# A one-core 4096 x 4096 matmul with leaky ReLU: when a21's pieces are turned, where s3's quarter sums lie, and leaky on two row tiles at once

## The chip, the core and the metric

The kernel runs on one core of a Trainium2 chip. TensorE multiplies (128 rows of the contraction at a time, into PSUM banks of 128 x 512 fp32), VectorE adds, subtracts, transposes 32 x 32 blocks and applies leaky ReLU, ScalarE copies PSUM banks to SBUF and squares blocks for a check, and the queues of GpSimd (POOL), SyncE (SP) and ScalarE issue transfers. The metric is the device time of one execution in microseconds. Three runs of the kernel before took 1546.32 to 1549.6 us, median 1548.78.

## The reference

```python
def reference(a, b, alpha):            # a, b: 4096 x 4096 float32, alpha = 0.01
    x = np.matmul(a, b)
    return np.where(x > 0, x, alpha * x)
```

## The kernel before

The output is cut into four row groups g (1024 rows) and four column blocks j (1024 columns), so 16 regions of 1024 x 1024. Region (0,0) is made by an ordinary product while data comes in. Each of the other fifteen, in the list `regions` (L489), is made by Winograd's form of Strassen's scheme: `a` and `b` of the region are split into 2 x 2 blocks, and seven products of sums replace eight. `PRODUCTS` (L636) names their left sides in order: a11, a12, s2, s3, s1, a22, s4. In the text, product 0 is a11, product 3 is s3, product 6 is s4. One such product is 64 matmuls of 128 x 512 (four row tiles, two halves k of the contraction, eight chunks). The order within a group is j = 2, 0, 1, 3, in group 2 it is 2, 0, 3, 1, and in group 0 it is 1, 2, 3.

The sums on the `b` side (t1 to t4, L571) are made in place on VectorE in every region. Those on the `a` side (s1, s2, s3, s4, L541) are made once per group, and s3 lies in the room of a21.

In most regions of groups 1 to 3 the last two products, and product 3 from a group's second region on, are split once more: seven quarter products of 16 matmuls of 128 x 256 replace 64 matmuls by 112 half-wide ones (L735). Their left sides need four quarter sums each. For a22 and s4 these are made in the group's first region and kept in DRAM (`kept_q`). For s3 they are made in the group by `sums_of_s3` (L708): sums 1 and 3 at the end of the first region, 2 and 4 in the second one (L996), in the rooms of quarters that are not needed meanwhile (`s3_rooms`, the x21 quarters of a22, s4 and s3), the fourth in a small tile and then in DRAM (`kept_s3`). From the second region on the fourth is loaded (L1060) into `t`, a tile that takes the room of s2 after product 2. The quarter sums of `b` for product 3 (`tq`: 2, 4 and 1) are made after product 1, in three small tiles (tag a16, of which there are three).

The last region of a group (`turning`: (0,3), (1,3) and (2,1)) is not made in quarters. In it the next group's `a` is fetched and turned: a11 after product 0, a12 after product 1 or 2, a21 after product 3, a22 after product 5, each block in four pieces. A piece is fetched by four casting transfers on POOL into an a16 tile (L131), turned by two 32 x 32 transposes on VectorE (L140) and squared on ScalarE by four instructions that also sum (L590); the row sums feed a check of the input's range (`note_rows`, L596). The squares of blocks of `b` (`Measure`, L229 to L262) feed the same check: three squares on ScalarE in `begin`, and in `end` a sum on VectorE, a fourth square, two more sums and a fold of five small steps. In (1,3) and (2,1) the block B22 is measured in the room of the next group's s2 (`IN_ROOM`). Since the quarter sums have overwritten x21 of a22, s4 and s3, these three quarters are reloaded from DRAM there (`load_x21`, L706).

What is done with the results: after product 0 ScalarE copies the y banks to u1 (L798), after product 1 VectorE adds the z banks (L942), makes the four row tiles leaky (L309) and SP stores them (L947): that is `leave`. After product 2 the y banks, which go on accumulating, are copied to u2. After product 3 the z banks are copied to v; after product 4 the y banks are added to v, which then leaves; after product 5 the z banks are added to u2; after product 6 the y banks are copied to kept_c (L1154) and leave. Products 5 and 6 go on accumulating in z and y, and the next region's products 0 and 1 start anew in the banks z and y of this one.

The schedule is written out by hand: each engine's queue runs its instructions in the order of the program's text and waits at semaphores. SP's order in a turning region is: u1's stores, x21 of s3, the loads of the next region's B12 (for groups 2 and 3 its finished sum t3), x21 of a22 and s4, v's stores, then the next region's B11 (two loads, L512), its B21, u2's stores, its B22, kept_c's stores. In the regions with j = 2 of groups 1 to 3, `b` is read from a 16-bit copy in DRAM (`kept`) on SP; in the others it comes from the input with a cast, on POOL (L515). ScalarE's copies of the z banks after product 3 stand behind the squares of a12's pieces.

## Time and profile before

| what | us |
|---|---|
| median of three runs (lowest to highest) | 1548.78 (1546.32 to 1549.6) |
| profiled execution, its own time | 1553.42 |
| its span, first to last instruction | 1551.6 |
| TensorE busy | 1528.9 (99%) |
| VectorE busy | 1148.7 (74%) |
| ScalarE busy | 425.1 (27%) |
| POOL busy | 300.4 (19%) |

The granted TensorE clock is 0.998 over the span. DMA moved 341 MB, mean 220 GB/s. In the rows of a timeline the columns are: start in us, length in us, engine and line, operation, output and inputs, shapes, count, and in brackets the engine's idle time before the row and what ended it. In the list of waits the columns are: who, what ended the wait, us in total, times, the longest. A group's row gives busy us and the mean ns of one instruction.

### The profile page before, as it was taken

How to read it: one execution, taken by the hardware profiler on the slowest of the kernel's cores; microseconds unless marked ns; L12 is line 12 of the kernel's file. 1: busy time of each engine (PE TensorE's matmuls, PEld its weight loads, DVE VectorE, ACT ScalarE, POOL GpSimd, SP SyncE). 2: the span in 40 equal slices, each digit the busy share in tenths (PEclk: the TensorE clock that was granted, in tenths of full speed). 3: DMA queues.
4: the chain of work that ended last, by engine and by line, in shares of the span. 5: the costliest groups of instructions: out<-in, count | busy, mean ns of one | idle time of the engine just before them, and what ended most of it. 6: DMA issues, size and time to landing. Idle time of an engine off the chain costs nothing. (4 is left out here: it accounts for less than half of the span.)

```text
span 1551.6 us, 21870 instructions
## 1 busy us (share of the span) xinstructions
PE 1528.9 (99%) x8571; PEld 836.8 (54%) x8571; DVE 1148.7 (74%) x1318; ACT 425.1 (27%) x730; POOL 300.4 (19%) x482
## 2 busy tenths in 40 slices
PE   9999999999999999999999999999999999999997
PEld 4444444444446466574444747557444475747656
DVE  4368768777797787966789698675869868787686
ACT  2201224646310214104651130311473113021310
POOL 5641110144102011023400202012340110201100
PEclk9999999999999999999999999999999999999999
DMA  9999695999879989599997979969999795979933
GB/s 244 182 215 199 129 286 156 180 197 187 271 279 276 217 189 277 145 267 201 230 305 252 282 175 228 240 166 274 207 204 342 201 282 138 273 193 189 273 109 139
DMA packets 218163, 341.30 MB, mean 220 GB/s; under 512 B 19137, under 2 KB 162753, under 8 KB 210114
## 3 DMA queue, kind: packets, MB, share of 16 engines
q0 software_dynamic: 149376, 141.59, 57.3%
q1 hardware_dynamic: 62050, 172.65, 30.3%
q10 hardware_dynamic: 6624, 25.56, 4.4%
q8 instruction: 69, 1.13, 0.3%
q14 instruction: 44, 0.36, 0.1%
HBM read 375.92 MB, written 103.29 MB: 309 GB/s over the span
## 5 line engine op out<-in xcount | busy, mean ns | idle before, releaser
L785 PE MATMUL ps<-b,a 128*128 128x512 f16 x2752 | 599.5, 379 | 6.0 <-DMA a<-kept_xs 4.4
L785 PE MATMUL ps<-b,s 128*128 128x512 f16 x2240 | 489.2, 379 | 1.4 <-DVE b L571 1.4
L785 PEld LDWEIGHTS <-a 128*128 128x128 f16 x2752 | 269.0, 98 | 330.2 <-DMA a<-kept_xs 5.3
L785 PEld LDWEIGHTS <-s 128*128 128x128 f16 x2240 | 219.1, 98 | 264.4 <-issue 1.8
L515 POOL DMA_DIRECT2D b<-in_b_dram x184 | 136.6, 747 | 920.1 <-PE ps L735 442.3
L571 DVE TENSOR_TENSOR b<-b 128x4096 f16<-128x4096 f16 x104 | 234.5, 2288 | 78.3 <-DMA b<-in_b_dram 70.9
L798 ACT COPY c<-ps 128x512 f32<-128x512 f32 x152 | 78.5, 596 | 452.6 <-PE ps L785 437.1
L140 DVE STREAM_TRANSPOSE a<-a 128x512 uint32<-128x512 uint32 (+2 forms) x120 | 126.8, 1105 | 92.3 <-DMA a<-in_a_dram 92.2
L131 POOL DMA_DIRECT2D a<-in_a_dram x252 | 137.8, 553 | 206.0 <-ACT junk L590 86.8
L590 ACT ACTIVATE junk<-a 128x512 bf16<-128x512 f16 x192 | 121.3, 632 | 111.4 <-DMA a<-in_a_dram 106.0
L309 DVE SCALAR_TENSOR_TENSOR c<-c 128x512 f32<-128x512 f32 x240 | 149.5, 686 | 3.1 <-ACT c L1154 3.0
L735 PEld LDWEIGHTS <-q 128*128 128x128 f16 x1392 | 135.8, 98 | 17.5 <-DMA q<-kept_s 1.6
L942 DVE TENSOR_TENSOR c<-ps,c 128x512 f32<-128x512 f32 x142 | 88.9, 683 | 59.6 <-PE ps L785 50.2
L229 ACT ACTIVATE sq<-b 128x2048 bf16<-128x2048 f16 x56 | 104.4, 1910 | 59.9 <-DVE sq L238 40.1
L281 PE MATMUL ps<-b,a 128*128 128x512 f16 x512 | 113.1, 379 | 2.4 <-DMA b<-in_b_dram 1.2
L735 PEld LDWEIGHTS <-a 128*128 128x128 f16 x1040 | 101.8, 98 | 15.4
L735 PE MATMUL ps<-b,q 128*128 128x256 f16 x752 | 88.2, 273 | 0.8 <-DMA q<-kept_s 0.8
L281 PEld LDWEIGHTS <-a 128*128 128x128 f16 x512 | 49.7, 98 | 63.7 <-issue 4.0
L883 ACT COPY c<-ps 128x512 f32<-128x512 f32 x9 | 5.3, 587 | 268.6 <-PE ps L735 148.3
L735 PE MATMUL ps<-b,a 128*128 128x256 f16 x656 | 77.2, 273 | 0.0
L836 DVE TENSOR_TENSOR c<-ps,c 128x512 f32<-128x512 f32 x80 | 52.3, 685 | 14.6 <-PE ps L735 14.6
L735 PEld LDWEIGHTS <-s 128*128 128x128 f16 x592 | 57.9, 98 | 6.7
(113 smaller groups left out, 892.0 us busy)
## 6 DMA issues: line engine op xcount, KB each, us to landing
b<-in_b_dram POOLq DMA_DIRECT2D x192, 512.0 KB, 13.5
out_dram<-c SPq DMA_DIRECT2D x240, 256.0 KB, 6.5
a<-in_a_dram POOLq DMA_DIRECT2D x244, 128.0 KB, 5.4
b<-kept SPq DMA_DIRECT2D x20, 1024.0 KB, 9.3
q<-kept_qs ACTq DMA_DIRECT2D x40, 512.0 KB, 7.9
s<-kept_s SPq DMA_DIRECT2D x18, 1024.0 KB, 6.4
q<-kept_qa SPq DMA_DIRECT2D x28, 512.0 KB, 7.3
b<-in_b_dram POOLq DMA_DIRECT2D x24, 256.0 KB, 9.3
```

Of the source, the lines that this page charges most:

```text
L131: nc.gpsimd.dma_start(a16[32 * q:32 * q + 32], src.rearrange("(g i) w -> i g w", i=32))
L140: nc.vector.transpose(part.rearrange("p c m e -> p c (m e)").bitcast(U32) .rearrange("p c (g i) -> p g c i", i=32), src[:, :, i * n:(i + 1 ...
L229: nc.scalar.activation(to, self.parts[n], SQUARE)
L281: nc.tensor.matmul(ps, a_cols(at[0, h, u], c, mt, (h, u) == (0, 0)), bt[0, u, nt][:, c, :], start=first, stop=last,)
L309: nc.vector.scalar_tensor_tensor(t, t, alpha, t, op0=MULT, op1=MAX if alpha <= 1 else MIN)
L515: nc.gpsimd.dma_start(t[:, c:c + 4, :], b_rows(j, u, c, 4, nt, g > 0))
L571: nc.vector.tensor_tensor(f(to), f(x0), f(x1), op)
L590: nc.scalar.activation(junk, piece[:, q, :], SQUARE, accum_out=to[:, 4 * n + q:4 * n + q + 1])
L735: nc.tensor.matmul(to[m], xq[:, c // 2, rows, c % 2], yq[:, c, :], start=first and c == 0 and m < banks, stop=c == KC - 1, skip_group_chec ...
L785: nc.tensor.matmul(banks[mt], a_cols(t, c, mt, t is first_a), B(half, nt, k)[:, c, :], start=first and (k, c) == todo[0], stop=(k, c) == t ...
L798: nc.scalar.copy(kept[mt], banks[mt])
L942: nc.vector.tensor_add(to, bank, to)
```

## The change

It has these parts.

- `leave` takes pairs of row tiles (a tile of 128 x 2 x 512) and makes both leaky in one instruction of 128 x 1024; the two stores stay separate. The addition of v to u2 in the quartered regions goes by pairs too.
- s3's fourth sum no longer goes through `t`. In a group's second region it is made after product 1 in an a16 tile (`sx4`), stored in DRAM and used from there; in later regions it is loaded into such a tile behind u1's stores. The second sum is made ahead of the early measures of that region.
- The quarter sum t1 moves from an a16 tile to `t`, and is made after product 2.
- In (1,3) and (2,1), s3's x21 is loaded before a11's pieces are fetched, ahead of u1's stores in SP's queue.
- In a turning region a21's pieces 3 and 4 are fetched with the others, but turned and squared after v has left. In (1,3) and (2,1) the measure of B22 moves from behind product 4 to behind product 3: its three squares stand ahead of piece 1, its end between pieces 1 and 2, and the rooms of the next s2 and s1 are taken in this order.
- a22's piece 4 is turned ahead of the sums s1 and s2 as before, but squared after product 6's copies, which now use `keep`.

```diff
-    def sums_of_s3(g, some):
+    def sums_of_s3(g, some, room=None):
...
             if n == 4:
-                sx[4] = by_chunk(new_a16())
+                sx[4] = by_chunk(room)
...
-                nc.sync.dma_start(by_chunk(kept_s3), sx[4])
+                nc.sync.dma_start(kept_s3, room)
...
-        def leave(acc, h, nt):
-            for mt, t in enumerate(acc):
-                leaky(t)
-                nc.sync.dma_start(place(g, h, mt, j, nt), t)
+        def leave(pairs, h, nt):
+            for r, t in enumerate(pairs):
+                leaky(t.rearrange("p m n -> p (m n)"))
+                for m in range(2):
+                    nc.sync.dma_start(place(g, h, 2 * r + m, j, nt), t[:, m, :])
...
-        def fetch_a(h, half, some=slice(None)):
-            if not turning:
-                return
-            for n in range(MT)[some]:
-                if n == 0:
-                    coming["rows", h, half] = small_pool.tile([P, 16], FP32, name="rows", tag=f"rows{half}")
-                fetch, turn = coming[h, half][n]
-                fetch()
-                turn()
-                square_rows(turn.held[0], n, coming["rows", h, half])
-                if n == MT - 1:
-                    rows_made.append(coming["rows", h, half])
+        def fetch_a(h, half, n):
+            if n == 0:
+                coming["rows", h, half] = small_pool.tile([P, 16], FP32, name="rows", tag=f"rows{half}")
+            coming[h, half][n][0]()
+
+        def square_a(h, half, n):
+            square_rows(coming[h, half][n][1].held[0], n, coming["rows", h, half])
+            if n == MT - 1:
+                rows_made.append(coming["rows", h, half])
+
+        def bring_a(h, half, some=range(MT)):
+            if turning:
+                for n in some:
+                    fetch_a(h, half, n)
+                    coming[h, half][n][1]()
+                    square_a(h, half, n)
...
         product(0, y, True)
+        if second_of_group:
+            sums_of_s3(g, (2,))
         for n, m in enumerate(early):
             if n:
                 m.begin()
             m.end()
-        if second_of_group:
-            sums_of_s3(g, (2, 4))
...
-        fetch_a(0, 0, slice(3 if g else None))
+        if turning and g:
+            load_x21(g, "s3")
+        bring_a(0, 0, range(3 if g else 4))
 
         product(1, z, True)
         add(u1, z)
-        leave(u1, 0, 0)
+        leave(u1_pairs, 0, 0)
...
         if in_fourth:
-            tq = {n: new_a16() for n in (2, 4, 1)}
+            tq = {n: new_a16() for n in (2, 4)}
+            sx4 = new_a16()
+            if not second_of_group:
+                nc.sync.dma_start(sx4, kept_s3)
             t3_of_b(quarters_of_b(i, 0, 1))
-            sums_of_b(quarters_of_b(i, 0, 1), tq)
+            sums_of_b(quarters_of_b(i, 0, 1), tq, (2, 4))
+            if second_of_group:
+                sums_of_s3(g, (4,), sx4)
...
-        if turning:
-            load_x21(g, "s3")
...
         u2_pairs, u2 = keep(y, 1 - side)
+        if in_quarters:
+            t = x_pool.tile([P, 4, QUARTER], DT, name="q", tag="x")
+        if in_fourth:
+            tq[1] = t[:, 3]
+            sums_of_b(quarters_of_b(i, 0, 1), tq, (1,))
...
-        if in_quarters:
-            t = x_pool.tile([P, 4, QUARTER], DT, name="q", tag="x")
-            if in_fourth:
-                nc.sync.dma_start(t[:, 3], kept_s3)
...
-        fetch_a(1, 0)
-        note_rows(1)
+        in_room = None
         if turning:
+            room = new_s(g + 1, "s2").rearrange("p k c m e -> p (k c m e)").bitcast(BF16)
+            if (g, j) in IN_ROOM:
+                in_room = measure(i, *IN_ROOM[g, j], room.rearrange("p (n w) -> p n w", n=4))
+                in_room.begin()
+            bring_a(1, 0, [0])
+            if in_room:
+                in_room.end()
+            bring_a(1, 0, [1])
+            for n in (2, 3):
+                fetch_a(1, 0, n)
             load_x21(g, "a22")
             load_x21(g, "s4")
...
-            for mt in range(MT):
-                nc.vector.tensor_add(u2[mt], u2[mt], v[mt])
+            for to, more in zip(u2_pairs, v_pairs):
+                f = lambda t: t.rearrange("p m n -> p (m n)")
+                nc.vector.tensor_add(f(to), f(to), f(more))
...
         product(4, y, False)
-        in_room = None
         if turning:
             new_s(g + 1, "s1")
-            t = new_s(g + 1, "s2").rearrange("p k c m e -> p (k c m e)").bitcast(BF16)
-            if (g, j) in IN_ROOM:
-                in_room = measure(i, *IN_ROOM[g, j], t.rearrange("p (n w) -> p n w", n=4))
-                in_room.begin()
...
             add(v, y)
-            leave(v, 1, 1)
-        if in_room:
-            in_room.end()
-        note_rows()
+            leave(v_pairs, 1, 1)
+        if turning:
+            for n in (2, 3):
+                coming[1, 0][n][1]()
+                square_a(1, 0, n)
+            note_rows(1)
...
-        fetch_a(1, 1, slice(3))
-        leave(u2, 1, 0)
+        bring_a(1, 1, range(3))
+        leave(u2_pairs, 1, 0)
...
-        fetch_a(1, 1, slice(3, None))
         if turning:
+            note_rows()
+            fetch_a(1, 1, 3)
+            coming[1, 1][3][1]()
             for name in ("s1", "s2"):
                 sum_a(g + 1, name)
...
-            _, kept_c = new_c(side)
-            for mt in range(MT):
-                nc.scalar.copy(kept_c[mt], y[mt])
+            kept_c, _ = keep(y, side)
+            if turning:
+                square_a(1, 1, 3)
             leave(kept_c, 0, 1)
```

## The prediction

> **What bounds the kernel now.** I read the busy table first, then TensorE's list of waits, then TensorE's timeline product by product, then the other engines' timelines in the two regions where most is lost.
>
> ```profile
> PE 1528.9 (99%) x8571; PEld 836.8 (54%) x8571; DVE 1148.7 (74%) x1318; ACT 425.1 (27%) x730; POOL 300.4 (19%) x482
> ```
>
> TensorE is the bound, and the change removes no matmul. So all it can win is TensorE's idle time, which its waits name (who, for what: us in total, times, longest):
>
> ```profile
> PE ps L785 <- DMA a<-kept_xs: 4.4, 2, 2.5
> PE ps L785 <- DVE b L571: 1.4, 1, 1.4
> ...
> PE ps L785 <- DMA b<-kept: 0.9, 1, 0.9
> ...
> PE ps L735 <- DMA q<-kept_s: 0.8, 2, 0.5
> PE ps L785 <- ACT c L1154: 0.3, 1, 0.3
> ```
>
> The timeline gives each wait its place. In region (2,1), where group 3's `a` is turned, products 3, 4, 5, 6 and the next region's product 0 begin thus:
>
> ```profile
> 1112.65 7.50 PE L785 MATMUL ps<-b,a 128*128 128x512 f16 x34
> 1122.66 6.65 PE L785 MATMUL ps<-b,a 128*128 128x512 f16 x30 [2.51 <-DMA a<-kept_xs]
> 1129.15 13.98 PE L785 MATMUL ps<-b,s 128*128 128x512 f16 x64
> 1142.96 13.98 PE L785 MATMUL ps<-b,a 128*128 128x512 f16 x64
> 1156.78 13.98 PE L785 MATMUL ps<-b,s 128*128 128x512 f16 x64
> 1171.68 18.52 PE L785 MATMUL ps<-b,a 128*128 128x512 f16 x85 [0.93 <-DMA b<-kept]
> ```
>
> An undisturbed product takes 13.81 us from start to start (1129.15 to 1142.96), in quarters 12.23. What exceeds that is lost: product 3 of (2,1) 2.69, of (1,3) 2.02, both for s3's x21; product 0 of (3,2) 1.09, for `b<-kept`; around product 1 of (2,2) 1.33, for the copies of L1154; product 2 of (2,0) 1.52, for the sums of L571; product 3 of (1,0), (1,1), (3,0) 0.15, 0.66, 0.48, for the fourth sum read back. Together 9.9 us, 0.6%. Last, what VectorE, ScalarE and SyncE's queue do behind product 3 of (2,1):
>
> ```profile
> 1139.83 2.03 ACT L798 COPY c<-ps 128x512 f32<-128x512 f32 x4
> 1155.11 7.30 ACT L229 ACTIVATE s<-b 128x2048 bf16<-128x2048 f16 x4
> ```
> ```profile
> 1151.12 2.10 DVE L140 STREAM_TRANSPOSE a<-a 128x512 uint32<-128x512 uint32 x2 [0.41 <-DMA a<-in_a_dram]
> 1153.15 0.30 DVE L596 TENSOR_TENSOR stats<-stats,rows 128x16 f32<-128x16 f32 x3
> 1153.38 2.47 DVE L942 TENSOR_TENSOR c<-ps,c 128x512 f32<-128x512 f32 x4
> 1155.77 2.48 DVE L309 SCALAR_TENSOR_TENSOR c<-c 128x512 f32<-128x512 f32 x4
> ...
> 1162.44 1.23 DVE L241 TENSOR_TENSOR s<-s 128x2048 bf16<-128x2048 bf16 x1 [0.57 <-ACT s L229]
> ...
> 1166.08 0.34 DVE L262 TENSOR_TENSOR stats<-stats,r 128x16 f32<-128x16 f32 x3
> ```
> ```profile
> 1156.47 2.67 SPq L947 DMA_DIRECT2D out_dram<-c  x4
> 1159.38 2.47 SPq L512 DMA_DIRECT2D b<-kept  x4
> ```
>
> The reader should see a chain: v is added and made leaky (L942, L309), only then can its stores issue, and only behind them in the queue the loads of B11 that product 0 of the next region waits for.
>
> **The change, part by part.** The sum is made against the profiled execution (span 1551.6, its time 1553.4 us), which lies 4.6 us above the median 1548.78; I carry the difference over to the median.
>
> *s3's x21 earlier, (1,3) and (2,1).* Its four loads leave their place behind u1's stores (issued at 734.4 and 1114.8) and follow s2's reload at 713.7 and 1093.1, 20 us earlier. With the observed 7.8 to 12.1 us to landing they are there before product 3 starts (733.7, 1112.65). Gain 2.02 + 2.69, if nothing takes its place. Price: 0.5 MB beside the fetches of a11's pieces; at the 408 GB/s of the busiest stretch that is 0 to 1.3 us for those. Their turns feed u1's last addition, ready at 731.3 and needed at 734.3: the 3 us cover it. Beyond that cover product 3 would start late by the rest.
>
> *The squares of a22's last piece behind the copies of product 6.* In (1,3) the copies ran at 804.7, after squares whose piece landed at 801.7, while product 6 ended at 791. Put ahead, they run some 10 us earlier: gain 1.33.
>
> *The B22 measure and a21's last two pieces.* This is the part that decides. Before, VectorE turned all four pieces, then added v and made it leaky, and the measure came last (the rows above). Now v has ahead of it: piece 1, the whole measure, piece 2; only pieces 3 and 4 go behind. The work in front grows a little: two pieces less (4.2 us), against three sums of 1.23 and a fold of 2.7 us (L241's end to L262's). But the measure waits for ScalarE, whose order is now: the copies of z (756.60 + 2.03 in (1,3), 1139.83 + 2.03 in (2,1); they stand behind the squares of a12's last piece, which waits for its landing), three squares of B22 (three quarters of 7.30, 5.5), piece 1's squares (3.0), the fourth square (1.9). So L241 runs 10.4 us after z's copies, at 769.0 and 1152.3. Then 4.0 to the fold's end, 2.1 for piece 2, 2.4 for the additions, 1.2 for the first leaky pair: the first store of v issues 9.7 later, at 778.7 and 1162.0, where it stood at 775.85 and 1156.47. It is 2.9 and 5.5 us later, although TensorE now comes 2.0 and 2.7 us sooner.
>
> Behind these stores wait the loads of B11. Product 0 takes first the half that is loaded second; in (2,1) it was released 15.1 us after v's first store (1156.5 to 1171.6), in (0,3), with no other fetching, it landed 12.9 after (389.8 to 402.7). Less of a22 is now being fetched meanwhile, so I take 13.5: 792.2 and 1175.5. The landing of a12's last piece also shifts, since the second t3 load now issues 2.0 and 2.7 us earlier and meets its fetch: 0 to +2, I take +0.9 and +0.5. Product 0 then starts at 793.1 in (2,2) and 1176.0 in (3,2). Before it was 790.97 and 1171.68: +2.1 and +4.3. In this the x21 gains and the 1.09 are already swallowed; z's copies, which would hold product 5 of (2,1) by 1 us (1140.4 to 1141.9 against a start of 1140.3), hide in the same wait. With the copies' 1.33 off, the turning regions together cost +0.8 +4.3 = +5.1. Ends: with 12.9 and no shift +2.5, with 15.1 and +2 and +1 +9.9.
>
> The Trainium skill, "DMA: Bandwidth & Descriptors", section "Anatomy of one DMA", fits a transfer as 2.0 us plus bytes over 436 GB/s (for GpSimd's path). An estimate from it: the two halves land some 6.8 us after issue, near 10.5 after v's first store, and the turning regions would come to about -0.9 instead of +5.1. The trace disagrees: its loads of this kind take 6.3 to 17.0, median 9.3.
>
> In (0,3) there is no such measure; v comes earlier and product 0 of (1,2) has 11 us to spare: 0.
>
> *The fourth sum and t1.* (2,0): the fourth sum's 1.23 leaves the chain ahead of the sums of L571; the second sum only moves to the front of the same ScalarE-fed measures. Product 2 gains 1.2 of 1.5. (1,0), (1,1): the sum stays in its room, or is loaded from behind u1's stores, one product earlier: 0.15 + 0.66 gained. (3,0): VectorE is late there for another reason (the b load that landed at 1289.65), and u1's addition starts at 1301.49. Behind it now: 2.4, leaky 2.3, t3 and two sums 3.75, the fourth sum: ready at 1311.1, needed by the third quarter product at 1306.65 + 3.5 = 1310.1. Then two L571 of 2.2 and t1, ready 1316.8, needed 1316.4. Lost 1.0 + 0.4 instead of 0.48: +0.9. In other regions t1 is ready before its place (+8.7 in product 3); at worst 1.2 each. Sum -1.1, between -2.5 (all gained) and +1.
>
> *leaky and u2 + v in pairs.* One 128x1024 costs 1.23 (the row of L309 on `part`) for two of 0.69 that overlap to 1.20 (four in 2.49). About 0.07 a pair saved on VectorE, 8 us in all, off the path; first stores of a leave issue 0.5 later, counted above. 0, at most 1 either way. The three reads of kept_s3 that go, and the moved row statistics: 0.
>
> Sum: +5.1 - 1.1 = +4.0, rounded with 0.2 for the pairs to +4.2: 1553.0 us.
>
> **Rivals.** *All stalls go (the other side).* If a12's last piece landed 3 us earlier in (1,3) and 7 to 8 in (2,1), v's stores would go out at 775.5 and 1154.4 and B11 be there in time. Then 2.02 + 2.69 + 1.09 + 1.33 + 1.1 = 8.2 are won: 1540.6. For it: 0.5 MB no longer load beside a12's pieces (734 to 746, DMA share 1.08). Against: that piece's fetch waits for a room that VectorE's turn frees at 746.5, whatever the load.
>
> *The loads are quicker.* (0,3)'s first half landed 7.3 us after issue behind its stores. If the second half now does, 11 after the first store, product 0 starts at 790.6 and 1173.5; the sum is -0.4 - 1.3 + 1.8 - 1.1 = -1.0: 1547.8. The Trainium skill's fit ("DMA: Bandwidth & Descriptors", "Anatomy of one DMA") is of this kind. Against: four loads and four stores then share the engines as before.
>
> *More contention.* The upper ends hold: +9.9 and +1: 1559.7. For it: the window 1164 to 1172 already runs at a DMA share of 1.01.
>
> **How the numbers follow.** Forecast case 0.50, its own range 1550 to 1556; all stalls go 0.20; quicker loads 0.17; more contention 0.13. No change means within 3.1 us (0.2%), about what a measurement can tell. Faster: 0.20 + 0.04 from quicker loads. Same: 0.13 + 0.09 from the forecast's lower part. Slower: the rest, 0.54. The range 1542 to 1559 cuts the outer half of the first and of the last rival.
>
> **What would show it.** Right: in (1,3) and (2,1) product 3 is one row of 64 without a wait; VectorE's L942 follows L262 and two turns; TensorE waits 3 to 8 us for `b<-kept` at product 0 of (2,2) and (3,2); L571's 1.4 shrinks to about 0.3; product 3 of (3,0) waits for VectorE's L718 and L674. Wrong: no wait on `b<-kept`, or v's stores before 776 and 1157.

## The result and the profile after

The changed kernel takes 1564.02 us (median of five runs, 1562.19 to 1566.1) against 1548.78 (1546.32 to 1549.6): 1.010 times as long, with a 95% interval of 1.0086 to 1.0115. The forecast was 1553.0, with a range of 1542 to 1559. So it is slower, as forecast, but by 15.2 us instead of 4.2, outside the range. The profiled execution after took 1564.15 us (span 1562.4).

The busy table of the changed kernel shows no more matmuls than before. TensorE is busy 6 us longer with the same 8571:

```profile
PE 1535.1 (98%) x8571; PEld 838.1 (54%) x8571; DVE 1138.7 (73%) x1179; ACT 424.3 (27%) x730; POOL 300.4 (19%) x482
```

Its list of TensorE's waits (what ended them: us in total, times, longest) has lost x21 (`a<-kept_xs`), L571 and the fourth sum's load (`q<-kept_s`), and has two new heads:

```profile
PE ps L785 <- DVE c L942: 7.3, 5, 3.3
PE ps L785 <- ACT c L798: 4.6, 4, 2.2
...
PE ps L785 <- DMA b<-kept: 0.4, 1, 0.4
...
PE ps L735 <- DVE q L718: 0.3, 1, 0.3
```

TensorE's timeline in (2,1) of the changed kernel, products 3, 4, 5, 6 and the first two of (3,2):

```profile
1115.70 13.98 PE L785 MATMUL ps<-b,a 128*128 128x512 f16 x64
1129.51 13.98 PE L785 MATMUL ps<-b,s 128*128 128x512 f16 x64
1145.67 14.79 PE L785 MATMUL ps<-b,a 128*128 128x512 f16 x64 [2.18 <-ACT c L798]
1163.80 0.38 PE L785 MATMUL ps<-b,s 128*128 128x512 f16 x1 [3.34 <-DVE c L942]
...
1165.59 15.01 PE L785 MATMUL ps<-b,s 128*128 128x512 f16 x61 [0.22 <-DVE c L942]
1180.96 13.99 PE L785 MATMUL ps<-b,a 128*128 128x512 f16 x64 [0.36 <-DMA b<-kept]
1195.87 14.79 PE L785 MATMUL ps<-b,a 128*128 128x512 f16 x64 [0.92 <-ACT c L798]
```

Product 3 is one row without a wait, as forecast. But product 6 waits 3.34 us for L942, the four additions of v, and then again before its second, third and fourth matmul. The reason is in the code: `add(v, y)` reads the y banks, and product 6 accumulates in those same banks. It may not write a bank until VectorE has read it. VectorE's timeline shows why the additions are late:

```profile
1146.00 2.10 DVE L140 STREAM_TRANSPOSE a<-a 128x512 uint32<-128x512 uint32 x2 [1.51 <-DMA a<-in_a_dram]
1150.72 1.23 DVE L238 TENSOR_TENSOR s<-s 128x2048 bf16<-128x2048 bf16 x1 [2.62 <-ACT s L229]
...
1157.19 1.23 DVE L241 TENSOR_TENSOR s<-s 128x2048 bf16<-128x2048 bf16 x1 [3.45 <-ACT s L229]
...
1160.84 0.34 DVE L262 TENSOR_TENSOR stats<-stats,r 128x16 f32<-128x16 f32 x3
1161.10 2.07 DVE L140 STREAM_TRANSPOSE a<-a 128x512 uint32<-128x512 uint32 x2
1163.09 2.45 DVE L942 TENSOR_TENSOR c<-ps,c 128x512 f32<-128x512 f32 x4
```

Piece 1 of a21 is turned at 1146.00; then come the measure's sums, which wait for ScalarE's squares; then piece 2; then the additions. VectorE is idle for most of 1148 to 1157. ScalarE in the same stretch: z's copies, behind the squares of a12's last piece, then B22's squares (its squares of a21's piece 1 lie in the gap between the last two rows):

```profile
1145.05 2.03 ACT L798 COPY c<-ps 128x512 f32<-128x512 f32 x4
1146.95 5.54 ACT L229 ACTIVATE s<-b 128x2048 bf16<-128x2048 f16 x3
...
1155.26 1.90 ACT L229 ACTIVATE s<-b 128x2048 bf16<-128x2048 f16 x1
```

POOL's timeline shows a second effect. There are three a16 rooms for pieces, and a room is free only when VectorE has turned and ScalarE has squared what lies in it. The fetch of a21's last piece waits 8.06 us for ScalarE (L590 is the square of a piece's rows). The next one waits 5.92, for the room of piece 2; ScalarE had squared that piece by 1160.0 and VectorE turned it only by 1163.2, so this wait is VectorE's, whatever the row names:

```profile
1145.44 2.15 POOL L131 DMA_DIRECT2D a<-in_a_dram  x4 [2.56 <-ACT junk L590]
1155.65 2.15 POOL L131 DMA_DIRECT2D a<-in_a_dram  x4 [8.06 <-ACT junk L590]
1163.72 2.15 POOL L131 DMA_DIRECT2D a<-in_a_dram  x4 [5.92 <-ACT junk L590]
```

So the transfers nearly stop, and then all come at once. In the windows of the changed kernel the columns are the stretch, its length, each engine's busy time, then the granted clock of TensorE, the DMA share and GB/s:

```profile
1148.00:1154.00 6.00, 6.00 (x29) 2.73 (x28) 2.55 (x3) 5.94 (x8) 0.00 (x0) 1.00 0.44 65
1154.00:1160.00 6.00, 6.00 (x29) 2.74 (x28) 2.71 (x4) 5.87 (x13) 2.15 (x4) 1.00 0.51 76
1160.00:1166.00 6.00, 1.99 (x8) 0.58 (x6) 5.93 (x12) 5.75 (x17) 2.15 (x4) 0.99 0.23 29
1166.00:1178.00 12.00, 12.00 (x49) 5.13 (x48) 10.42 (x15) 2.96 (x9) 4.30 (x8) 0.86 1.00 297
```

The last window has a clock of 0.86, and two shorter ones show it plainly, in (1,3) and in (2,1), right after product 6's wait:

```profile
780.00:782.00 2.00, 2.00 (x6) 0.76 (x5) 2.00 (x3) 0.16 (x2) 0.00 (x0) 0.50 1.11 160
1166.00:1168.00 2.00, 2.00 (x6) 0.74 (x5) 2.00 (x3) 0.07 (x1) 0.00 (x0) 0.50 1.11 150
```

While it is 0.50, matmuls start 427 ns apart instead of 216.

The table gives, for six products of each turning region's end, what each lasts beyond 13.81 us from its start to the next product's start, all from the starts of the products in the traces. "p0" and "p1" are the next region's first two.

| kernel | (1,3): 3, 4, 5, 6, p0, p1 | (2,1): 3, 4, 5, 6, p0, p1 | sum |
|---|---|---|---|
| before, profile of the prediction | 2.03, 0, 0, 0, 0.52, 0.81 | 2.69, 0, 0, 1.09, 0.02, 0 | 7.2 |
| after | 0, 0.67, 4.32, 3.07, 1.18, 0.81 | 0, 2.35, 4.32, 3.36, 1.10, 0.82 | 22.0 |

After, 4.6 of the 22.0 are product 5 and z's copies: 3.0 of waiting (under 4), and 0.81 in each region under 5, where its first four matmuls step behind the four copies (its row lasts 14.79 us instead of 13.98). The y banks take the other 7.0 under 5 and, in product 6, 1.15 in each region for the three short waits. Half clock takes 1.9 and 1.7 (matmuls 427 instead of 216 ns apart), the wait for B11 0.5, and p0 and p1 another 3.9, mostly for product 6's copies, which ScalarE makes only behind squares of a22's late pieces. Elsewhere the change won what it should: in (2,0) product 2 starts 1.40 sooner after the start of product 1, product 3 of (1,1) and (1,0) is 0.66 and 0.15 shorter, and product 3 of (3,0) is 0.31 longer.

### The profile page after: what moved, and what is told of

Same layout as the page of the kernel before. It is cut to its first block, busy times and chain, and to the rows that moved or that the text cites. A ratio compares the mean times of both kernels' runs of the same rounds, so it can differ in the third digit from the quotient of the medians.

```text
span 1562.4 us, 21610 instructions
## 1 busy us (share of the span) xinstructions
PE 1535.1 (98%) x8571; PEld 838.1 (54%) x8571; DVE 1138.7 (73%) x1179; ACT 424.3 (27%) x730; POOL 300.4 (19%) x482
## 5 line engine op out<-in xcount | busy, mean ns | idle before, releaser
L785 PE MATMUL ps<-b,s 128*128 128x512 f16 x2240 | 494.3, 381 | 7.4 <-DVE c L942 7.3
L785 PEld LDWEIGHTS <-a 128*128 128x128 f16 x2752 | 269.0, 98 | 332.1 <-issue 10.4
L571 DVE TENSOR_TENSOR b<-b 128x4096 f16<-128x4096 f16 x104 | 235.1, 2288 | 80.9 <-DMA b<-in_b_dram 71.6
L798 ACT COPY c<-ps 128x512 f32<-128x512 f32 x172 | 88.6, 596 | 448.2 <-PE ps L785 397.5
L590 ACT ACTIVATE junk<-a 128x512 bf16<-128x512 f16 x192 | 121.1, 631 | 138.4 <-DMA a<-in_a_dram 113.4
L309 DVE SCALAR_TENSOR_TENSOR c<-c 128x1024 f32<-128x1024 f32 (+1 forms) x121 | 141.4, 1209 | 4.4 <-ACT c L798 4.2
L942 DVE TENSOR_TENSOR c<-ps,c 128x512 f32<-128x512 f32 x142 | 88.8, 683 | 49.2 <-PE ps L785 32.7
L883 ACT COPY c<-ps 128x512 f32<-128x512 f32 x9 | 5.3, 586 | 268.7 <-PE ps L735 179.0
L836 DVE TENSOR_TENSOR c<-ps,c 128x512 f32<-128x512 f32 x80 | 52.3, 685 | 14.8 <-PE ps L735 14.8
```

Source lines behind the costliest of these rows:

```text
L309: nc.vector.scalar_tensor_tensor(t, t, alpha, t, op0=MULT, op1=MAX if alpha <= 1 else MIN)
L571: nc.vector.tensor_tensor(f(to), f(x0), f(x1), op)
L590: nc.scalar.activation(junk, piece[:, q, :], SQUARE, accum_out=to[:, 4 * n + q:4 * n + q + 1])
L785: nc.tensor.matmul(banks[mt], a_cols(t, c, mt, t is first_a), B(half, nt, k)[:, c, :], start=first and (k, c) == todo[0], stop=(k, c) == t ...
L798: nc.scalar.copy(kept[mt], banks[mt])
L942: nc.vector.tensor_add(to, bank, to)
```

## The experiments

Theory Y: v's additions come late, and product 6 needs the y banks. Rival L: the earlier x21 delays a12's last piece, and all behind it. Every result is set beside runs of the kernel before on the same chip.

**The measure behind v (changed kernel, one part undone).**

```diff
-                in_room.begin()
-            bring_a(1, 0, [0])
-            if in_room:
-                in_room.end()
-            bring_a(1, 0, [1])
+            bring_a(1, 0, [0, 1])
...
             new_s(g + 1, "s1")
+        if in_room:
+            in_room.begin()
...
             note_rows(1)
+        if in_room:
+            in_room.end()
```

> The changed kernel with B22's measure alone put back behind v (its squares behind those of a21's second piece, its sums behind the turns of pieces 3 and 4); all else stays changed. Theory Y (product 6 accumulates in the y banks, which v's additions must read first; the measure ahead of them makes TensorE wait 3.3 us or more twice, and the clock is halved after that): product 6 waits no longer, its matmuls keep 216 ns, and 4.3 + 3.1 + 4.3 + 2.3 = 14 us come back: 1550, down to 1545 if the earlier x21 is then a gain. Rival L (s3's x21 loaded early delays a12's last piece, and so the copies of z and all behind them): the measure's place is not what costs, 1559 or more.

Measured: 1545.34 us against 1548.53, ratio 0.998 (0.997 to 0.9991). The place of the measure costs 18.7 us by the medians (1564.0 less 1545.3), 18.4 by the two distances from the kernel before, and the rest of the change is a small gain. Of the waits of products 3 to 6 and of the next region's first two, TensorE's list has one row left:

```profile
PE ps L785 <- ACT c L798: 2.3, 2, 1.4
```

What is left of the sum in the table is 4.3 us, all of it product 5 and z's copies. L alone can't be the cause of the loss.

**The block alone (kernel before, with the measure ahead of v and pieces 3 and 4 behind it).**

```diff
-        fetch_a(1, 0)
-        note_rows(1)
+        in_room = None
         if turning:
+            t = new_s(g + 1, "s2").rearrange("p k c m e -> p (k c m e)").bitcast(BF16)
+            if (g, j) in IN_ROOM:
+                in_room = measure(i, *IN_ROOM[g, j], t.rearrange("p (n w) -> p n w", n=4))
+                in_room.begin()
+            fetch_a(1, 0, slice(1))
+            if in_room:
+                in_room.end()
+            fetch_a(1, 0, slice(1, 2))
+            for n in (2, 3):
+                coming[1, 0][n][0]()
...
             leave(v, 1, 1)
-        if in_room:
-            in_room.end()
-        note_rows()
+        if turning:
+            for n in (2, 3):
+                coming[1, 0][n][1]()
+                square_rows(coming[1, 0][n][1].held[0], n, coming["rows", 1, 0])
+            rows_made.append(coming["rows", 1, 0])
+            note_rows(1)
...
+        note_rows()
```

> The kernel before with only the measure ahead of v and a21's pieces 3 and 4 behind it; x21, the sums, leaky and the copies stay as before. Theory Y: the whole loss is here, 1562 to 1568, with waits of product 6 for L942's additions in (1,3) and (2,1) and half clock behind them. Rival L: without the earlier x21 there is little loss, 1549 to 1553.

Measured: 1564.01, ratio 1.0103 (1.0088 to 1.0117): the whole loss, as theory Y had it, and L falls. But the waits aren't the ones it named. The head of TensorE's waits in this kernel:

```profile
PE ps L785 <- ACT c L1162: 8.3, 2, 4.3
PE ps L785 <- DMA b<-kept: 2.7, 2, 1.7
```

In (2,1) v's additions are in time for product 6, the second row:

```profile
1157.13 2.44 DVE L942 TENSOR_TENSOR c<-ps,c 128x512 f32<-128x512 f32 x4
1159.09 13.98 PE L785 MATMUL ps<-b,s 128*128 128x512 f16 x64
```

They come 40.7 us after the start of product 3, where the changed kernel has 47.4, because a12's last piece is there sooner (turned 19.7 us after that start instead of 26.5); in this rival L has its part. What waits is the next region: product 0 for B11, and product 1 for product 6's copies (L1162), which stand behind the squares of a22's pieces. In (2,1) those landed at 1183.4. The next region's first two products lose 12.4 us here, 3.9 in the changed kernel. So the lateness finds TensorE at another place, and the price comes out the same; theory Y names only one of them.

**Product 6's wait taken away, the rest left late.** v's additions go ahead of the measure's sums; leaky and the stores stay behind them.

```diff
             bring_a(1, 0, [0])
-            if in_room:
-                in_room.end()
-            bring_a(1, 0, [1])
-            for n in (2, 3):
+            if not in_room:
+                bring_a(1, 0, [1])
+            for n in ((1, 2, 3) if in_room else (2, 3)):
                 fetch_a(1, 0, n)
...
             add(v, y)
+            if in_room:
+                in_room.end()
+                coming[1, 0][1][1]()
+                square_a(1, 0, 1)
             leave(v_pairs, 1, 1)
```

> The changed kernel with v's four additions alone put ahead of the measure's sums (behind the turn of a21's first piece); leaky and v's stores, and the loads of B11 behind them, stay behind the measure and piece 2. It tells the two waits apart that v's lateness can cause. If the wait of product 6 for the y banks, with the half clock behind it, is what costs: product 6 starts on time, 13 us come back, 1551. If the prediction's own wait (product 0 of the next region for B11, behind v's stores) is as long and was only hidden by the other: product 6 starts on time, but product 0 of (2,2) and (3,2) waits 5 to 8 us for b<-kept, with half clock after it, and the time stays at 1560 to 1565.

Measured: 1563.21, ratio 1.0094 (1.008 to 1.0109). That is no gain beyond the spread (the profiled execution, 1559.74, is the fastest of its four). Product 6 starts on time, and product 0 of (2,2) and (3,2) then waits 5.84 and 6.51 us for B11. The rows are TensorE's timeline and a window of this kernel:

```profile
773.51 13.98 PE L785 MATMUL ps<-b,s 128*128 128x512 f16 x64
793.33 30.72 PE L785 MATMUL ps<-b,a 128*128 128x512 f16 x128 [5.84 <-DMA b<-kept]
```
```profile
794.00:797.00 3.00, 3.00 (x8) 1.06 (x7) 0.00 (x0) 0.00 (x0) 0.54 (x1) 0.50 1.06 344
```

This is the wait that the prediction named. In the changed kernel it was hidden behind the wait for the y banks, and it takes over when that one goes. Either way product 0 starts at the same place: 35.1 and 35.7 us after the start of z's copies here, 35.6 and 35.9 in the changed kernel. The half clock behind the wait costs 2.9 and 1.9 us here.

**Filling the idle time.** Two kernels keep TensorE busy with matmuls of zeros, added to a bank that they don't change. The first does so behind product 5 of the changed kernel:

```diff
             product(5, z, False)
+            if in_room:
+                for _ in range(12):
+                    nc.tensor.matmul(z[0], w[:, :P], w, start=False, stop=True, skip_group_check=True)
```

> The changed kernel with 12 matmuls of zeros (2.6 us) added to bank z[0] behind product 5 in (1,3) and (2,1), so that TensorE is idle some 0.8 us instead of 3.3 while it waits for v's additions. If the idle time itself halves the clock: product 6's first matmuls take 216 instead of 427 ns, and 3.1 + 2.3 us are gained, 1559, or a little less of it where product 1 of the next region waits for the copies behind a22's squares. If the clock falls for another reason (the operands, the load of the transfers that start then): unchanged, 1564.

Measured: 1563.19, ratio 1.0092 (1.0079 to 1.0105): within the changed kernel's spread, so the 5 us didn't come. The mechanism did: at product 6 the idle time falls to 0.77 us, the clock stays at 1.00, and matmuls are 216 ns apart at once. In its timeline of (2,1), the first row is the zeros; below it, the window right after the additions:

```profile
1162.18 2.75 PE L1143 MATMUL ps<-w 128*128 128x512 f16 x12
1165.69 0.38 PE L785 MATMUL ps<-b,s 128*128 128x512 f16 x1 [0.77 <-DVE c L942]
...
1181.89 13.99 PE L785 MATMUL ps<-b,a 128*128 128x512 f16 x64 [1.08 <-DMA b<-kept]
```
```profile
1168.00:1170.00 2.00, 2.00 (x11) 0.90 (x10) 2.00 (x3) 0.00 (x0) 0.00 (x0) 1.00 1.08 165
```

The time won is given back at once: product 0 waits 2.25 us in (2,2) and 1.08 in (3,2) for B11. In (2,2) the half clock comes back as well, behind a wait of only 1.56 us for product 6's copies, and takes 1.7 us of product 1:

```profile
812.51 16.22 PE L785 MATMUL ps<-b,a 128*128 128x512 f16 x64 [1.56 <-ACT c L798]
```
```profile
813.50:816.90 3.40, 3.40 (x8) 1.07 (x8) 3.40 (x4) 3.21 (x9) 0.00 (x0) 0.50 1.16 339
```

The second kernel does the same behind product 6 of the kernel with the additions early, where B11 itself sets the end of the wait:

```diff
             product(6, y, False)
+            if in_room:
+                for _ in range(24):
+                    nc.tensor.matmul(y[0], w[:, :P], w, start=False, stop=True, skip_group_check=True)
```

> The kernel with v's additions early (1563.2), with 24 matmuls of zeros (5.2 us) added to bank y[0] behind product 6 in (1,3) and (2,1), so that TensorE is busy for most of its wait for B11. Product 0 starts when B11 has landed, as before. If the idle time halves the clock and nothing hides that here: the first product of (2,2) and (3,2) then takes 13.81 us from start to start instead of 16.74 and 15.69, 4.8 us less, 1558.4. If the half clock costs nothing in the end, because a later wait takes its place: 1563.

Measured: 1560.59, ratio 1.0083 (1.007 to 1.0097). Its timeline has the zeros, the short rest of the wait, and product 0 at full rate (13.99 for 64 matmuls):

```profile
789.76 5.34 PE L1176 MATMUL ps<-w 128*128 128x512 f16 x24
795.92 13.99 PE L785 MATMUL ps<-b,a 128*128 128x512 f16 x64 [0.82 <-DMA b<-kept]
```

Against the same kernel without zeros that is 1.3 us by the two distances from the kernel before (13.0 and 14.3), 2.6 by the medians, where 4.8 were expected. The intervals overlap. Both kernels show that it was the idle time that halved the clock at the place that they fill; what the half clock costs in the end, 1 to 3 us, is at the edge of what these runs can tell, since new waits for copies follow (0.69 us at product 1 of (2,2)).

**The measure's two halves apart.** First: the squares of B22 stay ahead on ScalarE, and only VectorE's sums go behind v.

```diff
                 in_room.begin()
-            bring_a(1, 0, [0])
-            if in_room:
-                in_room.end()
-            bring_a(1, 0, [1])
+            bring_a(1, 0, [0, 1])
...
             note_rows(1)
+        if in_room:
+            in_room.end()
```

> The changed kernel with the squares of B22 still ahead of a21's pieces on ScalarE, but the measure's sums on VectorE behind v and pieces 3 and 4. If the loss is VectorE's order (v waits behind sums that wait for ScalarE): as with the whole measure behind v, 1545 to 1546. If ScalarE's 5.5 us of squares ahead of the pieces' squares cost by themselves (rooms of a16 free later, a22's pieces later): 1548 or more.

Measured: 1564.75, ratio 1.0089 (1.0059 to 1.0119), with a wide spread (one run at 1548.2, the slowest 1570.6, the profiled one 1568.8). A surprise: the squares alone are enough. In (1,3), VectorE's and POOL's timelines of this kernel:

```profile
764.86 2.44 DVE L942 TENSOR_TENSOR c<-ps,c 128x512 f32<-128x512 f32 x4
...
783.37 2.11 DVE L140 STREAM_TRANSPOSE a<-a 128x512 uint32<-128x512 uint32 x2 [11.79 <-DMA a<-in_a_dram]
...
792.18 2.48 DVE L942 TENSOR_TENSOR c<-ps,c 128x512 f32<-128x512 f32 x4
```
```profile
769.17 2.15 POOL L131 DMA_DIRECT2D a<-in_a_dram  x4 [8.08 <-ACT junk L590]
```

v's additions are early (764.86). But the fetch of a21's piece 4 waits 8.08 us for the room of piece 1, which ScalarE squares behind B22. It then lands at 783.3 among v's stores and B11's loads. VectorE stands still for it, with the measure's sums and u2's additions (792.18) queued behind, and product 0 of (2,2) waits 6.9 us for those. Two more kernels test this reading.

The first puts piece 1's squares ahead of B22's in that kernel:

```diff
-                in_room.begin()
-            bring_a(1, 0, [0, 1])
+            bring_a(1, 0, [0])
+            if in_room:
+                in_room.begin()
+            bring_a(1, 0, [1])
```

> The kernel with B22's squares ahead and the measure's sums behind v (1564.8), with one change: the squares of a21's first piece stand ahead of B22's three on ScalarE. If the loss there comes from the rooms of a16 (the fetch of a21's piece 4 waits on POOL until ScalarE has squared piece 1, 5.5 us longer behind B22's squares, and then lands among v's stores and B11's loads): the fetch issues 5.5 us sooner, its turn no longer holds the measure's sums and u2's additions, 1545 to 1550. If something else in the squares costs (the port, the room s2): 1560 or more.

Measured: 1546.29, ratio 0.9992 (0.9981 to 1.0003). The four squares of one piece, 3 us of ScalarE, moved ahead of three others are worth 18 us. POOL's row for the same fetch in (2,1):

```profile
1140.25 2.15 POOL L131 DMA_DIRECT2D a<-in_a_dram  x4 [2.68 <-ACT junk L590]
```

The second makes the same exchange in the changed kernel, where the measure's sums stay ahead of v:

```diff
-                in_room.begin()
             bring_a(1, 0, [0])
             if in_room:
+                in_room.begin()
                 in_room.end()
```

> The changed kernel with the squares of a21's first piece ahead of B22's on ScalarE; VectorE's order stays as changed, and the last of B22's squares ends at the same time as before, so v's additions come no earlier. It takes away the longer hold of the rooms alone. If VectorE's order (v behind the measure) is enough for the loss: product 6 still waits 4.3 us with half clock after it, 1560 to 1564. If the rooms make most of it: a22's pieces and B11 land earlier, and only 4.3 + 1.5 to 3 us in each region stay over the kernel with the measure behind v, 1555 to 1558.

Measured: 1563.79, ratio 1.0092 (1.0079 to 1.0106). So VectorE's order is enough by itself, too: this kernel and the one before it differ only in whether the measure's sums stand ahead of v or behind it, and they are 17.5 us apart on the same chip. The head of TensorE's waits in this kernel:

```profile
PE ps L785 <- DVE c L942: 7.1, 4, 3.3
PE ps L785 <- ACT c L798: 4.8, 4, 1.8
```

Piece 4's fetch now waits only 2.67, but the one behind it 11.33 (POOL, 1166.78): it needs the room of piece 2, which VectorE turns only behind the measure, at 1164.15.

**The other parts, one at a time, on the kernel before.** x21 early:

```diff
+        if turning and g:
+            load_x21(g, "s3")
         fetch_a(0, 0, slice(3 if g else None))
...
-        if turning:
-            load_x21(g, "s3")
```

> The kernel before with only s3's x21 loaded early in (1,3) and (2,1). The prediction's step: product 3's waits of 2.0 and 2.5 us vanish and nothing takes their place, 1544. Rival L: a12's last piece lands up to 5 us later, and the copies of z hold product 5; a part or all of it is lost again, 1546 to 1553.

Measured: 1551.39, ratio 1.0018 (1.0009 to 1.0027): a small loss. Product 3's waits are gone, but product 6 is 1.36 and 1.06 longer before the next region starts (B11), and z's copies hold product 5 of (2,1) (0.96 and 0.81). Those copies start 26.0 and 28.0 us after product 3, against 21.8 to 23.1 in the two later profiles of the kernel before (below).

The fourth sum and t1 (the change's own lines for `sums_of_s3`, `sx4`, `tq` and `t`, nothing else):

> The kernel before with only the fourth sum of s3 and t1 in their new rooms and places. The prediction's step: 1.2 won in (2,0), 0.8 in (1,0) and (1,1), 0.9 lost in (3,0): 1547.4 against the kernel before at 1548.5. By the changed kernel's profile (1.40 + 0.15 + 0.66 won, 0.31 lost): 1546.6. Rival: the rooms or the load of the fourth sum make something else wait, 1548.5 or more.

Measured: 1546.60 against 1547.84, ratio 0.9988 (0.9979 to 0.9997). The step's 1.1 is 1.2.

Pairs in leaky and in u2 + v:

> The kernel before with only leaky and u2 + v on two row tiles at once. The prediction's step: nothing on the path, 1548.5, at most 1 either way. Rival: the first stores of each block issue 0.5 us later and B11's loads with them, which hold product 0 of (2,2) and (3,2): 1549 to 1550.

Measured: 1548.73, ratio 1.0004 (0.9993 to 1.0015): nothing.

**From the kernel with the measure behind v.** z's copies ahead of the squares of a12's last piece:

```diff
-        if g:
+        if turning and g:
+            bring_a(0, 1, range(3))
+            fetch_a(0, 1, 3)
+            coming[0, 1][3][1]()
+        elif g:
             bring_a(0, 1)
-        note_rows(1)
+        note_rows(0 if turning and g else 1)
...
             v_pairs, v = keep(z, side)
+            if turning and g:
+                square_a(0, 1, 3)
```

> The kernel with the measure behind v (1545.3), and besides in (1,3) and (2,1) the squares of a12's last piece behind the copies of z on ScalarE instead of ahead of them. If the copies of z hold product 5 only because those squares wait for the piece's landing: product 5 starts on time in both regions, 1.6 + 0.8 and 1.1 + 0.8 us come back, 1541. Rival: product 0 of (2,2) and (3,2) then waits for B11's loads, which come no earlier; half or less is won, 1543 to 1545.

Measured: 1542.66, ratio 0.9965 (0.9953 to 0.9978): faster than the kernel before by 5.2 us on the same chip, and 21.4 under the changed kernel's median. The sum of the table falls to 0.04 us. Its windows of (2,1), where the changed kernel's transfers had stopped:

```profile
1146.00:1152.00 6.00, 6.00 (x29) 2.71 (x28) 5.90 (x10) 5.84 (x13) 0.98 (x2) 1.00 1.00 303
1152.00:1158.00 6.00, 6.00 (x29) 2.74 (x28) 3.11 (x4) 5.84 (x14) 3.33 (x7) 1.00 1.03 369
```

x21 back at its old place, in the kernel with the measure behind v:

```diff
-        if turning and g:
-            load_x21(g, "s3")
         bring_a(0, 0, range(3 if g else 4))
...
+        if turning:
+            load_x21(g, "s3")
         if not g:
```

> The kernel with the measure behind v (1545.3), and besides s3's x21 loaded at its old place behind u1's stores. If the early load is worth what the prediction took (product 3 waits 2.0 + 2.5 us without it), less the 4.3 us that product 5 then waits for the copies of z: about the same, 1545 to 1547. If it costs by the traffic it puts beside a11's pieces, as the kernel before with the early load alone seems to say (1551.4 against 1548.5): 1542 to 1544.

Measured: 1544.45, ratio 0.9982 (0.9965 to 0.9999). No difference from 0.998. But z's copies move. The rows are theirs in (2,1), first with the early x21 (the measure behind v), then here:

```profile
1136.68 2.03 ACT L798 COPY c<-ps 128x512 f32<-128x512 f32 x4
```
```profile
1128.03 2.03 ACT L798 COPY c<-ps 128x512 f32<-128x512 f32 x4
```

From the start of product 3 in (1,3) and (2,1) that is 28.6 and 28.1 us with the early load and 21.4 and 21.2 without it, and it is all that the two kernels differ in. So the early load makes a12's last piece some 7 us later, and what it wins at product 3 goes at product 5. Whether it pays once z's copies no longer wait behind that piece was not tried: no run has the late load with z's copies first.

All four pieces of a21 ahead of v again, in the kernel with z's copies first:

```diff
-            bring_a(1, 0, [0, 1])
-            for n in (2, 3):
-                fetch_a(1, 0, n)
+            bring_a(1, 0)
...
-            for n in (2, 3):
-                coming[1, 0][n][1]()
-                square_a(1, 0, n)
             note_rows(1)
```

> The kernel with the measure behind v and z's copies first (1542.7), with all four pieces of a21 turned ahead of v again, as in the kernel before. If moving pieces 3 and 4 is what frees v's stores early enough: v's stores go 4.2 us later, product 0 of (2,2) and (3,2) waits up to 1 us each for B11, 1543 to 1545. If it is worth nothing: 1542.7.

Measured: 1545.90, ratio 0.9979 (0.9969 to 0.9989): product 6 grows by 2.48 and 1.32 until B11 is there; 0.8 of the first is two short waits for the y banks. Turning two pieces behind v seems to be worth some 2 us (0.9965 against 0.9979; the intervals overlap), the one part of the block that may do good.

**The kernel before, profiled twice more.**

> The kernel before, unchanged, profiled once more. If the prediction's sum failed in part because the one profiled execution (1553.4, 4.6 above the median) had stalls that most executions don't have: product 3 waits 1.3 to 1.6 us in (1,3) and 0.5 to 1.2 in (2,1), not 2.0 and 2.7, and around product 1 of (2,2) nothing is lost instead of 1.33. If they are the kernel's usual stalls: the same numbers again within 0.3.

> The same kernel a third time, for the spread of the same waits: as for the second look, product 3 of (1,3) and (2,1) waits 1.3 to 1.6 and 0.5 to 1.2 us if the first profile was untypical, 2.0 and 2.7 if it was not.

The profiled executions took 1549.21 and 1548.67 us (the prediction's profile: 1553.42). The x21 row of each one's waits, in this order, against 4.4 in the prediction's:

```profile
PE ps L785 <- DMA a<-kept_xs: 2.1, 2, 1.7
```
```profile
PE ps L785 <- DMA a<-kept_xs: 2.8, 2, 1.7
```

Product 3 lost 1.86 and 0.63 in the one, 1.28 and 1.92 in the other, and product 0 of (2,2) nothing in either. The sum of the table is 3.2 both times instead of 7.2. So the first profile was untypical, though not in every single wait.

## Why the prediction was wrong, step by step

That the change loses time, and that the place of the measure is why, was forecast and is so. The 11.0 us that were missed come from these steps.

**The step that failed: "The landing of a12's last piece also shifts ...: 0 to +2, I take +0.9 and +0.5".** The step counts all of v's lateness from z's copies on ScalarE, and these stand behind the squares of that piece. With the shift it has them 23.8 and 27.7 us after the start of product 3. In the changed kernel they start at 759.15 and 1145.05, 27.7 and 29.4 us after it: +4.8 and +2.2 against the prediction's profile, 5.5 us more than forecast in the two regions together. The early x21 does this, as the two kernels that differ in it alone show (28.6 and 28.1 against 21.4 and 21.2). The prediction priced its traffic for a11's pieces, at 0 to 1.3 us, and for a12's last one took too little. The condition "if nothing takes its place" failed with it: the waits at product 3 went, and product 5 waited 0.67 and 2.35 us for z's copies.

**From z's copies to product 0 the sum held, though not by the wait that it named.** It has 35.6 us (2.03 + 10.4 + 9.7 + 13.5); 35.6 and 35.9 were measured. L241 came 10.1 us after the end of z's copies in (2,1), where 10.4 were forecast. But TensorE did not spend this time waiting 3 to 8 us for `b<-kept`: that wait was 0.4, because TensorE was already late. "Behind these stores wait the loads of B11" was taken as the only thing that the late additions hold, and product 6, at the y banks, came first. For this wait the prediction had the rows and passed them over. That product 6 accumulates where L942 reads is in the code, and the profile of before shows the margin: L942 began at 1153.38, took 2.47, and product 6 began at 1156.78, 0.9 us later. The step put L942 at 1158.4 (1152.3 + 4.0 + 2.1), 5 us later, and never compared it with product 6. With the y banks out of the way, product 0 waits 5.84 and 6.51 us for B11, inside the forecast's 3 to 8, and starts no earlier. So the wait that was passed over moved TensorE's idle time and not the total. That the two waits end so close together is luck, for the step knew of one only.

**The copies of product 6: "gain 1.33".** By the sum nothing was to be lost at products 0 and 1 of the next region; 3.9 us were lost there. The copies left piece 4's squares behind, but the squares of three other pieces still stand ahead of them, and these pieces come late: in (2,1) the squares that the copies follow begin at 1189.35, and product 6 ends at 1180.6. In the kernel with the block alone this is the largest wait, 8.3 us at L1162. There x21 is not early, z's copies start 22.9 and 22.6 us after product 3, and the time is the same, 1564.0: what the first failed term adds in the one kernel, this second one adds in the other.

**The order on ScalarE was costed as time, not as a hold on rooms.** The step counted 5.5 us of squares ahead of piece 1's. It didn't ask who waits for piece 1's squares: POOL, with the fetches of the next pieces. The rooms, held by ScalarE and by VectorE, made the transfers stop at a share of 0.23 to 0.51 for 18 us, and run at 1.00 and more afterwards, with B11 and a22 in the same heap.

**The half clock** was in no step. In the changed kernel it made matmuls slower by 1.9 and 1.7 us. The Trainium skill, "TensorE: Matmul & The Clock Gate", Part 1, says that the clock falls to half after an idle window of about 3.4 us and that the window runs freely. The traces agree with the window: in every profile the stretches at 0.50 start on a grid of 3.41 us (in the changed kernel at 776.75 and 1165.87, 114 steps apart), and inside a run they last 3.41, 6.83 or 10.24 us. They differ on how much idle time it takes. Waits of 1.32 us (the changed kernel with piece 1's squares first), 1.56 (with the zeros) and 2.12 (with the squares ahead), each with short waits behind it, brought 0.50 as waits of 3.34 and more did, while one of 2.51 in the kernel before left the clock at 1.00. By the rows of all profiles, the grid step ahead of each of the 13 falls had at least 1.66 us without a matmul, and no step with more than 2.00 stayed without a fall. So in these runs the place of a wait on the grid counts beside its length.

**Carried to the median.** The sum was made against a profile 4.6 us above the median, and "I carry the difference over" assumed that its stalls are everyone's. They weren't: 7.2 us of stalls in that profile, 3.2 in the other two. The gains of 2.02 + 2.69 and 1.33 were counted on 4.0 us that the other two profiles don't lose. Its z's copies in (2,1) were late as well, 27.2 us after product 3 against 23.1 and 22.5.

**The smaller steps.** The fourth sum: forecast 1.1 gained, measured 1.2; the waits named for product 3 of (3,0) (L718, L674) were there, at 0.31 more instead of 0.9. Pairs: 0, measured 0. L571's 1.4 is gone from the list. The 408 GB/s were not those of the busiest stretch (422 between 782 and 792), which changes its term by less than 0.1.

**The sum.** Of the 11.0 us missed (1564.0 against 1553.0), the turning regions make 9.7: they lost 14.8 more than in the profile of before, and 5.1 were forecast. Of the 9.7, 5.5 are z's copies, 0.3 the way from there to product 0, and 3.9 products 0 and 1 of the next region. The carrying over makes 4.6. The fourth sum in the profiles takes 0.8 off, and the start and end of the two executions (1.4 and 0.7 shorter after) most of the rest.

**The rivals.** "More contention" was nearest in size, at 1559.7; it took +2 and +1 for the landing of a12's last piece, which moved by 4.8 and 2.2, and none of the rivals had product 6. The Trainium skill's fit for a transfer ("DMA: Bandwidth & Descriptors", "Anatomy of one DMA") stood behind the quicker loads, an estimate of 6.8 us for B11's two halves. With the additions early the half that released product 0 of (2,2) landed 12.7 us after its issue (780.6 to 793.3), so the traces still disagree, in a stretch with a DMA share of 1.07. "All stalls go", 1540.6, needed an earlier a12; the kernel with the measure behind v and z's copies first got to 1542.7 without it.

## What to carry to other kernels

When work is put ahead of an instruction, list everything that waits for that instruction and for each one queued behind it: the PSUM banks that it reads and someone will write, the rooms that it frees, the stores and loads behind it on its queue. Compare each with its margin in the trace; a margin of 0.9 us is a term of the sum. A transfer that is moved earlier is paid for by those that it now runs beside: find the last of them to land, and what stands behind it. Look at rooms as queues: three of them, freed by the slowest of two readers, turned a mere exchange of order on ScalarE into 18 us. And profile the kernel before more than once ahead of counting its stalls as gains.

## What the runs showed that was not expected

Waits lie behind one another here, and when one goes the next takes its time. Taking away the y-bank wait, the half clock at product 6 or the longer hold of piece 1's room alone gave 0.8, 0.8 and 0.2 us by the medians, all within the spread, of the 18.7 that putting the measure behind v gives.

A wait of 3.3 us cost more than its length: the clock was at 0.50 for 6.8 and 3.4 us, and matmuls of 128 x 512 came 427 ns apart instead of 216. Shorter waits did the same at some places, down to 1.32 us. Matmuls of zeros in the wait held the clock at 1.00 there. They pay only where no later wait takes the time back.
